# A two-layer decoder trunk on one core: the residual stream kept transposed, with weights as the stationary operand of the products that add to it

## The chip, the cores and the metric

The program runs on one core of one Trainium2 chip. The metric is the device time of one execution in microseconds (us). The kernel before takes 803.0 us, the median of three runs (802.51 to 804.0).

## The reference

Two consecutive layers act on a residual stream x of 256 tokens by 1,024 features, in float32. Each layer adds three branches to x, each behind an RMS norm with a gain: a token mixer, a cross-attention with 4 heads into 256 memory tokens, and a SwiGLU FFN of width 2,816. The mixer of layer 0 joins two kinds of sparse attention (8 heads each); that of layer 1 is grouped attention with a compressed, a selected and a window branch.

```
def rms_norm(x, gain):
    y = x * rsqrt(mean(x * x, axis=-1) + 1e-6)
    return y * gain

for each layer:
    x = x + mixer(rms_norm(x, norm_mix)) @ w_out
    x = x + mem_attention(rms_norm(x, norm_mem), rms_norm(mem, norm_mem_src)) @ mem_w_o
    g, u = split(rms_norm(x, norm_ffn) @ ffn_w_in)
    x = x + (silu(g) * u) @ ffn_w_out
```

## The kernel before

**Layout.** x lies in SBUF as two tiles (t = 0, 1) of 128 tokens on the partitions by 1,024 features. A product contracts over partitions, so a norm (`norm`, L619) transposes x: per half tile (512 features) TensorE makes four 128x128 transposes into PSUM, `evac_gain` (L608) multiplies the result by the gain on VectorE (tile `gv`), and splits it into a high part in fp32r (`move`: ScalarE or VectorE) and the low rest (`tt`: VectorE or GpSimd). The two parts stand in `hT`. The factor 1/rms is left out of the product's operand and applied to its result: ScalarE squares x with a running sum (tile `junk`), and `ms_root` (L599) makes mean and root of it. `mem_prep` (L1242) does the same with the memory tokens, in each layer anew, two tiles of 512 KB each.

**Products.** Each float32 product is three fp32r products (`mm3`, L565): high by high, high by low, low by high. `gemm` (L571) handles one tile of 128 tokens and a block of up to 512 weight columns: activations are the stationary operand (128x128), weights the moving one (up to 512 columns). Weights come by DMA in units of 256 rows by 512 columns (512 KB) into three raw buffers, and `pusher` (L395) splits each unit into high and low (tile `whl`, six units): the high part on ScalarE, the rest on VectorE. The products that add to x are `project` (L1375; twice 4 blocks of 128 rows), the end of `mem_attn` (L1292; 4 blocks) and the end of `ffn` (L1385; 22 blocks). Each of their results is 128 tokens by 512 features, and `residual` (L640) adds it to x on VectorE. `project` waits per half of the heads and per token tile for the attention's result (`finish`, L741, splits it, with `split`, L735), and `mem_attn` per pair of heads and per token tile.

**Order.** The program's order is made when it is built, by a planner: generators (`spawn`) yield operations, `Steps.run` (L84) takes the one that can start first by estimated costs and finish times (`Est`, L140), and operations that can run on several engines go to the one that would end first. Attention operations have rank 2, the main line of products rank 4, so the products fill what attention leaves free. Each engine then runs its list in that order. Buffers are slots (`Slots`, L263): two PSUM banks for products (`MM`), two each for scores, transposes and attention results, 23 slabs in SBUF. `main` (L1479) runs, per layer: mixer, keys of the memory (`mem_k`, L1267), `project`, `mem_attn`, `ffn`; the norms are spawned beside them and wait for the halves of x that they read.

The line that stops `project` before a token tile, and the adding of one result:

```
yield has(("oT", t, half), L + 1)
...
yield V.tensor_tensor(xs, ps, xs, op=OP.add)
```

Of the kernel before, what the change touches and what calls it, by code (L numbers as in the profile page):

```python
# [15 lines left out]
P = 128  # L16
D = 1024
# [122 lines left out]
class Est:  # L140
# [73 lines left out]
    class Engine:  # L214
# [21 lines left out]
        def cost(self, name, a, k, outs, ins):  # L236
# [3 lines left out]
            if self.n == "PE":  # L240
# [4 lines left out]
                if ins[0].dtype == F32R:  # L245
                    return n * (1 if n >= 256 else 4) * 0.000422
# [48 lines left out]
def trunk(ctx: ExitStack, tc: tile.TileContext, I, out):  # L295
# [42 lines left out]
    GV = Slots(est, tp, "gv", 2)  # L338
# [11 lines left out]

    x = [cp.tile([P, D], F32, name=f"x{t}") for t in range(NT)]
    xin = I["x"].rearrange("b (t p) d -> (b t) p d", p=P)
    rows = cp.tile([NG, P], F32, name="rows")
    posi = cp.tile([P, NT], I32, name="posi")

    def load_x(t, h, at):
        s = slice(512 * h, 512 * h + 512)
        nc.sync.dma_start(x[t][:, s], xin[t][:, s])
        est.note(x[t][:, s], est.wr, at, "D")

# [8 lines left out]
    def plan_block(key, w, col, n, K, base=0):  # L369
        plan_at[key] = len(plan)  # L370
        for k0 in range(0, K, 2):
            plan.append((w, col, n, base + k0))

    def load(i, lag=2.0):
        if i < len(plan):
            w, col, n, k0 = plan[i]
            raw, free = RW.take([P, 2, 512])
# [3 lines left out]
            nc.sync.dma_start(raw[:, :, :n], w[k0 * P:(k0 + 2) * P, col:col + n].rearrange("(k p) n -> p k n", p=P))  # L381
            raws[i] = (raw, free)

    class Unit:
        def __init__(self, i):
            n = plan[i][2]
            hl, self.free = WS.take([P, 2, 2, 512], F32R)
            self.hi, self.lo, self.n, self.left = hl[:, 0, :, :n], hl[:, 1, :, :n], n, NT
# [6 lines left out]
    def pusher():  # L395
        for i in range(len(plan)):
            yield WS.ready
            raw, rfree = raws.pop(i)
            u, n = Unit(i), plan[i][2]
            at[0] = i  # L400
            yield move(u.hi, raw[:, :, :n])
            yield V.tensor_tensor(u.lo, raw[:, :, :n], u.hi.bitcast(F32), op=OP.subtract)
# [13 lines left out]
    LASTC = 2  # L416
    for L in range(2):
# [3 lines left out]
        for half in (0, 1):  # L421
            for c in (0, 1):
                plan_block((L, "out", half, c), (I["ab_w_out"] if L == 0 else I["nsa_w_out"])[0], 512 * c, 512, 4, 4 * half)
        plan_block((L, "mq"), I["mem_w_q"][L], 0, 512, KD)
        plan_block((L, "mv"), I["mem_w_kv"][L], 512, 512, KD)
        for p in range(2):
            for c in (0, 1):
                plan_block((L, "mo", p, c), I["mem_w_o"][L], 512 * c, 512, 2, 2 * p)
# [4 lines left out]
        for k in range(0, KF - 2 * LASTC, 2):  # L433
            for c in (0, 512):
                plan.append((I["ffn_w_out"][L], c, 512, k))
        for c in (0, 512):
            for k in range(KF - 2 * LASTC, KF, 2):
                plan.append((I["ffn_w_out"][L], c, 512, k))
# [9 lines left out]
    load_x(0, 0, 3.5)  # L448
    nc.sync.dma_start(rows, I["gains"])
    est.note(rows, est.wr, 3.6, "D")  # L450
    load_x(0, 1, 4.4)
    clk["D"] = 3.3
    load(0, 1.1)
    load(1, 1.1)
    for h in range(2):
        clk["D"] += 0.73
        load_x(1, h, clk["D"] + 1.1)
    for i in range(2, RAWS):
        load(i, 1.1)
# [9 lines left out]
    gps, f = TP.take([P, 512])  # L469
    T.transpose(gps[:, :NG], rows, ident[:NG, :NG]).issue()  # L470
    gT = cp.tile([P, NG], F32, name="gT")
    V.tensor_copy(gT, gps[:, :NG]).issue()
    f()
# [12 lines left out]
    def tables():  # L486
# [21 lines left out]
        yield has(("mix0", 0), 2)  # L508
# [62 lines left out]
    def gemm(key, t, h, K, ev, need=None, part=None):  # L571
# [4 lines left out]
        for k0 in range(0, K, 2):  # L576
            u = yield from unit(plan_at[key] + k0 // 2)
            if need and k0 % 4 == 0:
                yield has(need[0], need[1] + 1 + k0 // 4)
# [11 lines left out]


    hT = [[cp.tile([P, KD, P], F32R, name=f"h{e}{t}") for e in range(2)] for t in range(NT)]
    junk = tp.tile([P, 512], F32, name="junk")
# [942 lines left out]
```

## Time and profile before

| | |
|---|---|
| median of three runs | 803.0 us (802.51, 803.0, 804.0) |
| profiled execution | 801.81 us, of which the span of the core is 800.1 us |
| granted clock of TensorE, mean | 0.996 |
| TensorE matmul busy | 766.0 us, 96% |
| VectorE busy | 537.5 us, 67% |
| ScalarE busy | 435.4 us, 54% |
| GpSimd busy | 130.9 us, 16% |
| read from HBM | 119.46 MB |

The span runs from the first instruction to the last; the profiled execution's own time is 1.7 us longer than it. Busy time of TensorE (PE) counts pipelined products and is no measure of its peak. PEld is its loading of stationary operands, DVE is VectorE, ACT ScalarE, POOL GpSimd, SPq the queue that issues DMAs. Most operations carry one line (L232), that of a helper, so groups are told apart by the names of their tiles: `mm` and `po` are PSUM banks with products, `sp` with scores, `tp` with transposes; `whl` are split weights, `h` the normed activations, `slab` other activations.

### The profile page before, as it was taken

The numbers are of one execution on the slowest core, as the hardware profiler recorded it, in microseconds if no ns is written. First come the engines' busy times: TensorE is split into PE (matmuls) and PEld (weight loads), VectorE is DVE, ScalarE is ACT, GpSimd is POOL, SyncE is SP. The second block draws the span as 40 slices with busy tenths as digits, with TensorE's granted clock in tenths as the row PEclk, the third lists the DMA queues.
The fourth block names the chain that finished last, engine by engine and source line by source line (L and its number), as shares of the span: only waits on it lengthen the run. The fifth ranks groups of instructions, "written<-read, shape, count | busy, mean of one in ns | idle before, by whom it ended". The sixth has DMA issues, their size and how long they took to land.

```text
span 800.1 us, 11833 instructions
## 1 busy us (share of the span) xinstructions
PE 766.0 (96%) x4259; PEld 632.1 (79%) x4259; DVE 537.5 (67%) x1096; ACT 435.4 (54%) x816; POOL 130.9 (16%) x192
## 2 busy tenths in 40 slices
PE   6878999999999999999999988999999999999998
PEld 5766777888888888888878776878897888889886
DVE  6779998877655655545727798887868565646541
ACT  5666887565544434444526788864656334435430
POOL 1544332110000000000007463230200000000000
PEclk9999999999999999999999999999999999999999
DMA  7613334635565553887315632033635656546761
GB/s 221 208 55 112 134 124 122 181 119 159 158 191 179 168 186 119 240 251 224 116 56 148 210 112 81 1 103 110 184 105 146 198 184 180 167 141 209 225 184 52
DMA packets 69482, 121.27 MB, mean 152 GB/s; under 512 B 8420, under 2 KB 15664, under 8 KB 69424
## 3 DMA queue, kind: packets, MB, share of 16 engines
q1 hardware_dynamic: 69392, 120.53, 49.2%
q8 instruction: 33, 0.54, 0.3%
q14 instruction: 25, 0.20, 0.1%
q0 software_dynamic: 32, 0.00, 0.0%
HBM read 119.46 MB, written 1.05 MB: 151 GB/s over the span
## 4 chain that ended last, share of the span: by engine, by line
PE 83%; DVE 7%; ACT 4%; DMA 2%; issue 2%; POOL 1%; SPq 0%; POOLq 0%; ACTq 0%; DVEq 0%
PE mm L232 61%; PE po L232 12%; PE tp L232 7%; PE sp L232 3%; DVE whl L232 2%; DMA raw<-in_ab_w_in 1%; DMA raw<-in_ffn_w_in 1%; ACT sn L232 1%; ACT whl L232 1%; DVE slab L232 1%; DVE acc L232 1%; ACT slab L232 1%; DVE sn L232 1%; DVE t L232 1%; POOL sn L232 1%
## 5 line engine op out<-in xcount | busy, mean ns | idle before, releaser
L232 PE MATMUL mm<-whl,h 128*128 128x512 f32 (+3 forms) x1776 | 397.8, 379 | 8.5 <-DVE whl L232 6.9
L232 PEld LDWEIGHTS mm<-whl,h 128*128 128x128 f32 x1776 | 310.8, 189 | 68.0 <-DVE whl L232 8.9
L232 DVE TENSOR_TENSOR whl<-raw,whl 128x1024 fp32r<-128x1024 f32 (+3 forms) x232 | 270.9, 1170 | 116.6 <-ACT whl L232 112.4
L232 ACT ACTIVATE whl<-raw 128x1024 fp32r<-128x1024 f32 (+3 forms) x211 | 213.2, 1014 | 160.1 <-DMA raw<-in_ffn_w_in 38.4
L232 PE MATMUL mm<-whl,slab 128*128 128x512 f32 (+1 forms) x840 | 200.2, 376 | 0.9 <-DVE x L232 0.8
L232 PEld LDWEIGHTS mm<-whl,slab 128*128 128x128 f32 x840 | 140.6, 189 | 27.7 <-issue 2.4
L232 PE MATMUL po<-whl,slab 128*128 128x512 f32 x264 | 68.4, 396 | 0.0
L232 ACT ACTIVATE slab<-tp 128x256 fp32r<-128x256 f32 (+2 forms) x63 | 28.3, 471 | 56.3 <-PE tp L232 55.9
L232 PEld LDWEIGHTS po<-whl,slab 128*128 128x128 f32 x264 | 49.4, 188 | 11.4
L232 POOL TENSOR_TENSOR rh<-vh,mhalf 128x1 f32<-128x1 f32 x12 | 9.5, 794 | 293.6 <-DVE vh L232 283.1
L232 ACT ACTIVATE sn<-sn,mx 128x128 f32<-128x128 f32 (+1 forms) x96 | 42.7, 447 | 6.9 <-DVE mx L232 6.5
L232 PE MATMUL tp<-ident,t 128*128 128x128 f32 x224 | 34.8, 277 | 2.7 <-DVE slab L232 2.3
L232 PE MATMUL tp<-ident,sn 128*128 128x128 f32 (+1 forms) x180 | 30.9, 281 | 4.8 <-POOL sn L232 3.8
L232 DVE TENSOR_TENSOR x<-mm,x 128x512 f32<-128x512 f32 x36 | 24.6, 687 | 16.0 <-PE mm L232 15.9
L232 PEld LDWEIGHTS tp<-ident,t 128*128 128x128 f32 x224 | 27.1, 142 | 9.6 <-DVE slab L232 2.8
L232 ACT ACTIVATE pt<-tp 128x512 f32<-128x512 f32 (+2 forms) x51 | 27.0, 536 | 13.7 <-PE tp L232 11.8
L232 DVE CUSTOM_DVE_ANT_0 sn<-sp,cm,rq 128x128 f32<-128x128 f32 (+1 forms) x80 | 30.5, 410 | 4.9 <-PE sp L232 3.8
L232 POOL TENSOR_TENSOR sn<-sn,rc 128x512 f32<-128x512 f32 (+2 forms) x27 | 25.5, 944 | 43.5 <-DVE rc L232 28.6
L232 ACT ACTIVATE t<-mm,rh 128x512 f32<-128x512 f32 (+1 forms) x26 | 17.0, 654 | 27.0 <-PE mm L232 27.0
L232 PEld LDWEIGHTS tp<-ident,sn 128*128 128x128 f32 (+1 forms) x180 | 20.7, 141 | 11.6 <-POOL sn L232 5.2
L232 ACT ACTIVATE t<-mm 128x512 f32<-128x512 f32 (+2 forms) x46 | 23.7, 553 | 10.0 <-PE mm L232 8.0
L232 DVE SCALAR_TENSOR_TENSOR t<-mm,rh,t 128x512 f32<-128x512 f32 (+1 forms) x24 | 16.9, 704 | 18.2 <-PE mm L232 18.2
(200 smaller groups left out, 676.3 us busy)
## 6 DMA issues: line engine op xcount, KB each, us to landing
raw<-in_ffn_w_in SPq DMA_DIRECT2D x80, 512.0 KB, 3.8
raw<-in_ffn_w_out SPq DMA_DIRECT2D x44, 512.0 KB, 4.5
raw<-in_ab_w_in SPq DMA_DIRECT2D x16, 512.0 KB, 3.9
raw<-in_mem_w_kv SPq DMA_DIRECT2D x16, 512.0 KB, 4.0
raw<-in_nsa_w_in SPq DMA_DIRECT2D x16, 512.0 KB, 3.7
raw<-in_ab_w_out SPq DMA_DIRECT2D x8, 512.0 KB, 3.6
raw<-in_mem_w_q SPq DMA_DIRECT2D x8, 512.0 KB, 4.2
raw<-in_mem_w_o SPq DMA_DIRECT2D x8, 512.0 KB, 3.6
```

Source lines behind the costliest of these rows:

```text
L232: return f(*a, **{q: v() if q in ("start", "stop") and callable(v) else v for q, v in k.items()})
```

## The change

x is kept as one tile of 128 features on the partitions by 8 blocks by 256 tokens; x, the memory tokens and the output are given in that layout in HBM (rearranged outside the kernel, once), and the gains also come transposed. A norm reads x directly: `gained` makes the high part (`move` with the gain as scale) and the rest (one `scalar_tensor_tensor`) per block of 256 columns. The sum of squares over features now runs over partitions: `squares` squares two blocks on ScalarE and adds them into `acc` (VectorE or GpSimd), and `ms_root` sums `acc` over partitions with two one-column products per norm. The memory's root is made once, in layer 0, and its tokens come in four pieces of 256 KB. The products that add to x take a 128x128 block of weights as the stationary operand and both token tiles (256 columns) as the moving one (`sums`): 1,632 products of 256 columns stand where 816 of 512 columns stood. Their weights come in units of 512 rows by 256 columns (`plan_banks`), also 512 KB, except those of the first part of the FFN's second product, which stay. A result is two blocks of features by 256 tokens, in one bank; the two head pairs of the memory's attention are now summed in PSUM. `project` and the memory's product wait for both token tiles of a half or pair. Two cost estimates of the planner are changed.

```diff
                 if ins[0].dtype == F32R:
-                    return n * (1 if n >= 256 else 4) * 0.000422
+                    return n * 0.00045 + 0.002
...
-            est.issue("D", [raw], [], 1.45 * n / 512)
+            est.issue("D", [raw], [], 2.4 * m * n / 1024)
...
+    def plan_banks(key, w, base):
+
+        plan_at[key] = len(plan)
+        for b in range(NB):
+            plan.append((w, 256 * b, 256, base, 4))
...
-    load_x(0, 0, 3.5)
+    clk["D"] = 1.2
+    nc.sync.dma_start(gT, I["gains_t"])
+    est.note(gT, est.wr, 3.4, "D")
+    for i in range(NB):
+        load_x(i)
+        if i < RAWS:
+            load(i, 1.1)
     nc.sync.dma_start(rows, I["gains"])
...
+    def sums(u, ps, k0, c0, hi, lo, first, last):
+
+
+        for k in range(2):
+            for j in range(2):
+                o, s = ps[:, j * SEQ:(j + 1) * SEQ], slice(c0 + j * P, c0 + (j + 1) * P)
+                whi, wlo = u.hi[:, k0 + k, s], u.lo[:, k0 + k, s]
+                yield T.matmul(o, whi, hi[:, k], start=first and k == 0 and j == 0, stop=False)
+                yield T.matmul(o, whi, lo[:, k], start=False, stop=False)
+                yield T.matmul(o, wlo, hi[:, k], start=False, stop=last and k == 1 and j == 1)
+                done("mm")
...
+    def gained(src, gain, hi, lo):
+
+        yield move(hi, src, gain)
+        yield V.scalar_tensor_tensor(lo, src, gain, hi.bitcast(F32), op0=OP.mult, op1=OP.subtract)
+
+    def squares(src, acc, first):
+
+        sq, f = yield from T2.get([P, 2, SEQ])
+        yield S.activation(sq, src, AF.Square)
+        if first:
+            yield tt(acc, sq[:, 0], sq[:, 1], OP.add)
+        else:
+            for j in range(2):
+                yield tt(acc, acc, sq[:, j], OP.add)
+        f()
+
+    def ms_root(key, acc, name):
...
+        ps, f = yield from TP.get([P, 512])
+        for t in range(NT):
+            yield T.matmul(ps[:, t:t + 1], acc[:, t * P:(t + 1) * P], one, start=True, stop=True)
+        yield V.tensor_scalar(v, ps[:, :NT], 1.0 / D, EPS, op0=OP.mult, op1=OP.add)
+        f()
         yield from pow_half(r, v)
...
-        for h in range(2):
-            yield has(("x", t, h), ver)
-            xs = x[t][:, 512 * h:512 * h + 512]
-            ps, f = yield from TP.get([P, 512])
-            for k in range(4):
-                yield T.transpose(ps[:, k * P:(k + 1) * P], xs[:, k * P:(k + 1) * P], ident)
-            yield from evac_gain(ps, f, hT[t][0][:, 4 * h:4 * h + 4], hT[t][1][:, 4 * h:4 * h + 4], gain[:, 4 * h:4 * h + 4])
-            done((key, t))
...
+    def norm(key, col, ver):
...
+        spawn(square())
+        for b in range(NB):
+            yield has(("x", b), ver)
+            for k in (2 * b, 2 * b + 1):
+                yield from gained(x[:, k], gT[:, col + k:col + k + 1], hT[0][:, k], hT[1][:, k])
+            done(key)
...
     def mem_prep(L):
...
+        for b in range(NB):
+            raw, rf = yield from T2.get([P, 2, SEQ])
+            nc.sync.dma_start(raw, I["mem"][:, 2 * b:2 * b + 2])
             est.note(raw, est.wr, clk["PE"] + 6.0, "D")
...
+            if L == 0:
+                yield from squares(raw, acc, b == 0)
             rf()
...
     def project(L):
         for half in range(2):
-            for t in range(NT):
-                yield has(("oT", t, half), L + 1)
-                hi, lo, f1, f2 = oT[t, half]
-                for c in range(2):
-                    yield from gemm((L, "out", half, c), t, lambda k: (hi[:, k, :], lo[:, k, :]), 4, residual(c))
...
+            for b in range(NB):
+                yield MM.ready
+                ps, free = MM.take([P, 512])
+                u = yield from unit(plan_at[L, "out", half] + b)
+                for i in range(2):
+                    yield has(("oT", L, half, i), 2)
+                    (hi, _), (lo, _) = oT[L, half][i]
+                    yield from sums(u, ps, 2 * i, 0, hi, lo, i == 0, i == 1)
+                u.free()
+                spawn(residual(b, ps, free))
...
+        for b0 in (0, 2):
+            held = []
+            for p in range(2):
+                yield has(("mo", L, p), 2)
+                for b in (b0, b0 + 1):
```

## Rows read from the trace of the kernel before

**Rows 1.** The page: engines, and the chain that ended last, by engine.

```profile
PE 766.0 (96%) x4259; PEld 632.1 (79%) x4259; DVE 537.5 (67%) x1096; ACT 435.4 (54%) x816; POOL 130.9 (16%) x192
PE 83%; DVE 7%; ACT 4%; DMA 2%; issue 2%; POOL 1%; SPq 0%; POOLq 0%; ACTq 0%; DVEq 0%
```

**Rows 2.** Stretches: PE, PEld, DVE, ACT, POOL busy; clock, DMA share, GB/s.

```profile
186.00:203.00 17.00, 16.41 (x79) 13.07 (x79) 15.69 (x23) 8.81 (x13) 0.00 (x0) 1.00 0.69 213
460.00:500.00 40.00, 34.35 (x297) 28.55 (x295) 35.43 (x138) 33.94 (x105) 20.97 (x26) 0.96 0.29 96
725.00:732.00 7.00, 7.00 (x62) 7.00 (x62) 3.64 (x6) 3.31 (x7) 0.00 (x0) 1.00 0.61 203
```

**Rows 3.** Whom TensorE waited for: us in total, times, longest.

```profile
PE tp L232 <- DVE slab L232: 5.6, 5, 2.0
```

**Rows 4.** The chain that ended last, in order of time: start, us, what.

```profile
203.24 0.44 PE tp L232 x4
203.68 13.75 PE mm L232 x60
...
724.38 8.25 PE mm L232 x70
...
790.69 5.61 PE po L232 x24
```

**Rows 5.** Groups of TensorE by shape: count, busy us, mean ns of one, idle before.

```profile
L232 PE MATMUL tp<-ident,x 128*128 128x128 f32 x96 | 15.8, 292 | 1.4 <-DMA x<-in_x 1.4
L232 PE MATMUL mm<-whl,slab 128*128 128x256 f32 x192 | 26.3, 285 | 0.0
L232 PE MATMUL sp<-kbd,slab 128*128 128x30 f32 x32 | 4.3, 265 | 0.0
```

**Rows 6.** Instructions in order of time at the program's start, TensorE.

```profile
3.99 1.06 PE L232 MATMUL tp<-ident,x 128*128 128x128 f32 x4
```

**Rows 7.** The same where layer 0's attention ends: start, us, engine.

```profile
138.86 0.66 PE L232 MATMUL po<-pt,bv 128*64 128x128 f32 x8
...
139.83 0.58 ACT L232 ACTIVATE slab<-po 128x512 fp32r<-128x512 f32 x1
139.96 1.23 DVE L232 TENSOR_TENSOR whl<-raw,whl 128x1024 fp32r<-128x1024 f32 x1 [0.30 <-ACT whl L232]
141.10 0.68 DVE L232 TENSOR_TENSOR slab<-po,slab 128x512 fp32r<-128x512 f32 x1
```

**Rows 8.** Output products after attention's end: layer 0 (139.4 to 151.9), layer 1 (543.9 to 561.3).

```profile
L232 PE MATMUL mm<-whl,slab 128*128 128x512 f32 x48 | 12.2, 402 | 0.0
...
L232 PE MATMUL mm<-whl,slab 128*128 128x512 f32 x69 | 17.0, 399 | 0.0
```

**Rows 9.** Groups of VectorE, ScalarE and GpSimd by shape, columns as in rows 5.

```profile
L232 DVE TENSOR_TENSOR x<-mm,x 128x512 f32<-128x512 f32 x36 | 24.6, 687 | 16.0 <-PE mm L232 15.9
L232 DVE SCALAR_TENSOR_TENSOR acc<-sn,iw,acc 128x256 f32<-128x256 f32 x7 | 3.7, 526 | 0.3 <-ACT sn L232 0.3
L232 DVE TENSOR_TENSOR slab<-po,slab 128x256 fp32r<-128x256 f32 x8 | 3.2, 418 | 3.7 <-ACT slab L232 3.7
...
L232 ACT ACTIVATE slab<-tp,kv 128x256 fp32r<-128x256 f32 x8 | 3.5, 473 | 5.5 <-PE tp L232 5.5
...
L232 POOL TENSOR_TENSOR acc<-acc,cmi 128x256 f32<-128x256 f32 x1 | 0.7, 737 | 3.3 <-DVE acc L232 3.3
```

**Rows 10.** One operation of VectorE beside GpSimd, and alone, in order of time.

```profile
206.75 0.69 DVE L232 CAST whl<-raw 128x1024 fp32r<-128x1024 f32 x1
...
467.70 1.73 POOL L232 TENSOR_TENSOR t<-t,t 128x512 fp32r<-128x512 f32 x1 [0.49 <-ACT t L232]
468.22 1.76 DVE L232 CAST whl<-raw 128x1024 fp32r<-128x1024 f32 x1
```

**Rows 11.** DMA: issues of the memory tokens in layer 1; landing times by size.

```profile
480.70 4.04 SPq L1246 DMA_DIRECT2D t<-in_mem  x2
...
raw<-in_ffn_w_in SPq DMA_DIRECT2D x8, 256.0 KB, 2.8
```

More of the change, by code (lines that the diff above doesn't have):

```diff
@@ new lines, in trunk @@
+    hT = [cp.tile([P, KD, SEQ], F32R, name=f"h{e}") for e in range(2)]
+    def hsel(t):
+        return lambda k: (hT[0][:, k, t * P:(t + 1) * P], hT[1][:, k, t * P:(t + 1) * P])
+    def gained(src, gain, hi, lo):
[10 more added lines that the diff above has]
+        f()
@@ L1288, in mem_k @@
         for t in range(NT):
-            yield has(("mT", L, t))
-            yield from gemm((L, "mk"), t, msel(t), KD, ev)
+            yield from gemm((L, "mk"), t, msel(t), KD, ev, ("mT", L))
     def mem_attn(L):
@@ L1345, in mem_pv @@
             ptf()
[L1346 to L1349 removed]
+            if (L, p) not in mo:
+                mo[L, p] = None
+                mo[L, p] = (yield from SL.get([P, 2, SEQ], F32R)), (yield from SL.get([P, 2, SEQ], F32R))
+            yield lambda: mo[L, p] is not None
+            yield from split(po, *(mo[L, p][e][0][:, :, t * P:(t + 1) * P] for e in range(2)))
+            pof()
+            done(("mo", L, p))
         def ev_v(p):
             def ev(ps, free, t):
[L1353 removed]
+                yield move(vm[:, t, 2 * p:2 * p + 2].rearrange("p h d -> p (h d)"), ps, (yield from root("mem", t))[1])
                 free()
@@ L1358, in mem_attn @@
         for t in range(NT):
[L1359 removed]
+            yield from gemm((L, "mq"), t, hsel(t), KD, ev_q, ("mem", L))
         for p in range(2):
@@ L1449, in ffn @@
-        n = 0
-        for i in range(KF // 2 - LASTC):
+        ps = []
+        for R in (MM, MM, PV, PV):
+            yield R.ready
+            ps.append(R.take([P, 512]))
+        n = plan_at[L, "fo"]
+        for i in range(KF // 2 - 2):
             yield has(("aT", L, i), 2)
             for c in range(2):
-                u = yield from unit(i0 + n)
+                u = yield from unit(n)
                 n += 1
-                for t in range(NT):
-                    yield from fo(u, i, c, t)
+                for b in range(2):
+                    yield from sums(u, ps[2 * c + b][0], 0, 256 * b, aT[i][0][0], aT[i][1][0], i == 0, False)
+                u.free()
@@ L1457, in ffn @@
             for e in range(2):
                 aT[i][e][1]()
-        for t in range(NT):
-            m = n
-            for c in range(2):
-                for i in range(KF // 2 - LASTC, KF // 2):
-                    yield has(("aT", L, i), 2)
-                    yield from fo((yield from unit(i0 + m)), i, c, t)
-                    m += 1
-                spawn(residual(c)(ps[t, c][0], ps[t, c][1], t))
-        for i in range(KF // 2 - LASTC, KF // 2):
+        for b in range(NB):
+            u = yield from unit(n + b)
+            for i in range(KF // 2 - 2, KF // 2):
+                yield has(("aT", L, i), 2)
+                yield from sums(u, ps[b][0], 2 * (i - KF // 2 + 2), 0, aT[i][0][0], aT[i][1][0], False, i == KF // 2 - 1)
+            u.free()
+            spawn(residual(b, *ps[b]))
```

271 lines of the change are left out of this document (110 added, 161 removed).

## The prediction

> **What bounds the kernel now.** I read the page's engines and its chain first, then the stretches, then the chain piece by piece, and the groups of each engine for prices. The page [rows 1] shows TensorE busy for 96% of the span, and the chain that ended last lies on TensorE for 83%. So a product or transpose taken from TensorE in a stretch where it is never idle is time won, and work taken from another engine is not. Where is it not full? The chain in order of time [rows 4] shows the FFN as products end to end, broken only by groups of four transposes. In layer 1's attention (460 to 500) it is busy 34.35 us of 40, so 5.65 us are idle [rows 2]. At the end of the memory's attention and the start of the FFN (186 to 203) it is nearly full, but VectorE is busy 15.69 us of 17 there: the engine to watch. The output products left after an attention's end [rows 8] show how much the main line has in hand when the attention stops: 48 of 96 in layer 0, 69 of 96 in layer 1.
>
> **The change part by part.** The sum is made against the profiled execution, 801.8 us, 1.2 us under the median of 803.0; I move the result up by that.
>
> *Transposes of norms.* The code has 16 transposes per norm in six norms; the group of x has these 96 [rows 5]. A group of four costs the chain 0.44 us [rows 4]. Five norms (both memory norms, both FFN norms, layer 1's mixer norm) lie in full stretches: 5 x 4 groups x 0.44 = **-8.8 us**. The sixth opens the program, see below. The memory tokens' 2 x 16 transposes go too. Layer 1's four groups lie where output products fill up: 4 x 0.44 = **-1.8**. Layer 0's four I cost at nothing: they lie ahead of an attention whose end sets when the second half of its output products can run.
>
> *Start.* Four transposes (1.06 us, [rows 6]) and a 128x512 multiply out of PSUM (0.69, as the residual's [rows 9]) no longer stand between the first x and its first product: **-1.8**. Against it, all of x (1 MB) must now land for the first token tile; before, half. Lower bound 0, upper bound twice the gain; I take the path's length.
>
> *Narrower products.* 816 products of 512 columns become 1,632 of 256. The old ones are priced by the FFN's last 24: 5.61/24 = 0.234 us each, 190.7 in all [rows 4]. The new by the 70 of 256 columns in the FFN's narrow block: 8.25/70 = 0.1179, 192.3 in all [rows 4]. Difference **+1.6**. The ends: 0 (two halves were nowhere cheaper than the whole), and the dearest row of this shape, 26.3/192 = 0.137 us [rows 5], which gives 223.6 and +32.9. That row's products lie among other work, so I stay with the unbroken run. There the loading of stationary operands is busy 7.00 us of 7.00 [rows 2]: no reserve is left.
>
> A rule of the Trainium skill speaks against this step: "TensorE: Matmul & The Clock Gate", section "Back-to-back issue gap", gives as the sustained spacing of load and product pairs 81 ns at 128 columns and 131 ns at 512. By it two narrow products cost at least 162 ns against 131, an estimate of 816 x 0.031 = +25 us for this term. The trace does not bear it out: 234 ns at 512.
>
> *Sums of squares.* Seven roots (six norms, the memory once) put 14 float32 products of one column on TensorE. The nearest row has 30 columns: 4.3/32 = 0.134 us [rows 5]; 14 x 0.134 = **+1.9**, between 0 and the price of a group of transposes per root (7 x 0.44 = 3.1).
>
> *Waiting for both token tiles.* In layer 0, 48 products remain when the attention ends, the whole second half [rows 8]; token tile 0's 24 hid the wait for tile 1. Now nothing does. After the last attention product (about 139.5), the copy started at 139.83 and the rest at 141.10, behind a weight split of 1.23 us [rows 7]. With half pieces (0.42 for the rest, [rows 9]; about as much for the copy) the first operand is ready at 140.7 without a split ahead, 141.5 with one: 1.2 to 2.0, taken **+1.6**. In layer 1, 69 remain, so 21 of the first half (21 x 0.234 = 4.9 us) cover the same 2 us. The memory's product waits likewise for tile 1's first pair, behind which the second pair's products run: 0.3 per layer, **+0.6**, between 0 and the 2.0 above per layer. The second pair is covered by 24 narrow products (2.8 us).
>
> *The norm after the last product.* The next gemm needs the last bank only after 18 products: 18 x 13.75/60 = 4.1 us [rows 4]. The bank needs the addition (0.69), high part (0.47) and two rests (2 x 0.53, [rows 9]): 2.2 us. It fits with 1.9 us in hand, one weight split but not two. For six boundaries I put in **+1.5**; alone it would be 0, the upper end is a rival below. VectorE loses 8 of 40 additions (5.5 us), 32 multiplies and their rests, and gains 64 rests (33.7) and up to 49 additions of 256 columns (49 x 0.418 = 20.5); about even. ScalarE's 64 scaled copies (30 us) replace squares with sums and unscaled copies of the same order, at 54% busy [rows 1].
>
> *Memory tokens.* SP now issues four pieces in place of two, among the weight loads behind it [rows 11]. Each piece lands in about 2.8 us [rows 11], but the planner reckons 6 us for each and takes the next one only after it. So layer 1's keys may start earlier (a quarter suffices) yet end no earlier. I put **-0.5**; between -5.65 (all idle time of 460 to 500 filled) and +1.7 (12 us later at that stretch's idle share, 14%). Weight units with rows of 1 KB in place of 2 KB cost nothing by the same landing time, half of a unit in 2.8 us against 2.8 us of products per unit, with three raw buffers ahead; if that cover is gone, about a microsecond per FFN.
>
> Sum: -8.8 - 1.8 - 1.8 + 1.6 + 1.9 + 1.6 + 0.6 + 1.5 - 0.5 = **-5.7**, so 796.1 for the profiled execution and **797.3 us** by the median.
>
> **The rivals.**
>
> *More comes back than the transposes.* The planner's costs are changed: 0.232 us in place of 0.216 for a product of 512 columns, nearer to the rows' 0.229 to 0.234, and a slower DMA. If instructions are then placed so that the three waits I added (3.7 us) vanish, and half of the 5.6 us in which transposes wait for VectorE [rows 3], the time is 797.3 - 3.7 - 2.8 = **790.8**. For it: the idle time exists. Against it: that order is the planner's and cannot be read from this trace.
>
> *The last bank's norm comes late (slower).* Per bank of 2.83 us of products, VectorE has a split (1.23), an addition (0.69), two rests (1.05) and two sums (0.84): 3.8 us, 1.0 too much. Over four banks it is 3.9 us behind, the operand comes 3.9 + 2.2 - 4.1 = 2.0 us late, at five boundaries 10 us; less the 1.5 already counted: **805.8**. It decides from (5.7 + 1.5)/5 = 1.4 us per boundary on. For it: VectorE's load at 186 to 203 [rows 2]. Against it: the sums may go to GpSimd, idle there [rows 2], at 0.74 us each [rows 9]. But one VectorE operation that takes 0.69 us alone took 1.76 beside a GpSimd one [rows 10], and the new rests read two operands from SBUF where the old multiply read PSUM. The Trainium skill, "SBUF — State Buffer", section "SBUF: two separate sides", tells of one port pair that a GpSimd operation and such a VectorE operation take in turn, whole; the trace agrees.
>
> *Weight loads set the pace (slower).* With the load queue full, any dearer load shows 1,632 times. At 0.137 us [rows 5] the time is 797.3 + 31 = **828**; from 0.1214 us on (5.7/1,632 more) the gain is gone. Against it: the unbroken run. The skill's spacing rule above, if it held, would end here, too.
>
> *Nothing to measure.* If the bounds above fall on the bad side (root products 3.1, layer 0's wait 2.0, memory waits 4.0, memory tokens +1.7), it is 797.3 + 7.2 = **804.5**.
>
> **How the numbers follow.** A measurement of this kernel can tell about 0.2% from no change, so faster means under 801.4 and slower over 804.6. Chances: the forecast 0.48, more coming back 0.27, nothing to measure 0.11, the late norm 0.11, weight loads 0.03. The first two are faster (0.75), the last two slower (0.14). The range 788 to 804 holds the forecast, most of the second and half of the third case.
>
> **What would show it.** Right: no transposes of x or of memory tokens, 1,632 products of 256 columns at 0.116 to 0.120 us in the FFN's second product, norm boundaries without idle time, a wait of 1 to 2 us before layer 0's second half. Wrong: TensorE waiting for `h` at each boundary, narrow products above 0.121 us apart, root products that stop TensorE, or a span under 790 with the attention stretches shortened.

## The result, and the profile after

The changed kernel takes **810.2 us** (median of 4 runs, 809.52 to 812.63) beside 802.8 of the kernel before on the same chip: a ratio of 1.0094, 95% interval 1.0070 to 1.0119. It is slower by 7.3 us, where 797.3 had been forecast. The profiled execution takes 810.7 us with a span of 809.0, beside 800.1 before.

The page of the changed kernel, its engines and the engines of the chain that ended last, beside [rows 1]:

```profile
PE 766.7 (95%) x4974; PEld 669.4 (83%) x4974; DVE 545.8 (67%) x1092; ACT 423.6 (52%) x803; POOL 166.6 (21%) x227
PE 82%; DVE 8%; ACT 5%; issue 2%; POOL 1%; DMA 1%; SPq 0%; ACTq 0%; POOLq 0%; DVEq 0%
```

TensorE is busy for as long as before (766.7 us against 766.0), in a span 8.9 us longer. So what was added is idle time; what the transposes gave back was taken up by other work on TensorE. The starts of the stages, from TensorE's instructions in order of time, say where (us):

| stage begins with | before | changed | late by | added in the stage before it |
|---|---|---|---|---|
| memory queries, layer 0 | 152.02 | 158.09 | 6.07 | 6.07 |
| FFN, layer 0 | 199.18 | 204.22 | 5.04 | -1.03 |
| FFN's second product, layer 0 | 325.54 | 331.18 | 5.64 | 0.60 |
| mixer, layer 1 | 388.49 | 394.74 | 6.25 | 0.61 |
| memory queries, layer 1 | 561.38 | 568.47 | 7.09 | 0.84 |
| FFN, layer 1 | 608.23 | 614.56 | 6.33 | -0.76 |
| FFN's second product, layer 1 | 734.57 | 741.49 | 6.92 | 0.59 |
| end of the span | 800.1 | 809.0 | 8.9 | 1.98 |

Two thirds are lost before layer 0's memory queries. Stretches of the kernel before, which show where (columns as in [rows 2]):

```profile
80.00:120.00 40.00, 38.22 (x247) 29.82 (x247) 36.25 (x122) 33.72 (x87) 14.90 (x20) 1.00 0.38 129
480.00:520.00 40.00, 36.74 (x334) 30.48 (x335) 34.46 (x150) 32.47 (x110) 12.65 (x17) 1.00 0.11 41
```

The same stretches of the changed kernel:

```profile
80.00:120.00 40.00, 30.37 (x199) 23.15 (x198) 33.84 (x136) 29.40 (x84) 15.65 (x22) 0.96 0.31 100
480.00:520.00 40.00, 35.21 (x318) 28.47 (x317) 32.60 (x144) 31.59 (x107) 18.68 (x23) 0.96 0.20 67
```

Beside layer 0's attention 9.6 of 40 us are idle on TensorE, where 1.8 were. What is missing there stands in the order of time. First SP's issues of the memory tokens, two tiles in the kernel before:

```profile
66.41 0.34 SPq L1246 DMA_DIRECT2D t<-in_mem  x1
85.46 0.41 SPq L1246 DMA_DIRECT2D t<-in_mem  x1
```

and four pieces in the changed kernel, the last one requested 19.5 us later than the last tile before:

```profile
70.16 0.42 SPq L1267 DMA_DIRECT2D t<-in_mem  x1
77.53 0.46 SPq L1267 DMA_DIRECT2D t<-in_mem  x1
89.13 0.50 SPq L1267 DMA_DIRECT2D t<-in_mem  x1
104.91 0.50 SPq L1267 DMA_DIRECT2D t<-in_mem  x1
```

Then TensorE's products of the memory keys (`mm<-whl,slab` of 512 columns), of the output projection behind them (`mm<-slab,whl`), and the first of the memory queries:

```profile
84.92 1.32 PE L233 MATMUL mm<-whl,slab 128*128 128x512 f32 x5
87.32 0.46 PE L233 MATMUL mm<-whl,slab 128*128 128x512 f32 x1
90.05 0.86 PE L233 MATMUL mm<-whl,slab 128*128 128x512 f32 x3
91.38 1.02 PE L233 MATMUL mm<-whl,slab 128*128 128x512 f32 x3 [0.47 <-ACT slab L233]
101.79 1.40 PE L233 MATMUL mm<-whl,slab 128*128 128x512 f32 x5
103.97 0.49 PE L233 MATMUL mm<-whl,slab 128*128 128x512 f32 x1
117.26 0.50 PE L233 MATMUL mm<-whl,slab 128*128 128x512 f32 x1
...
133.43 3.02 PE L233 MATMUL mm<-slab,whl 128*128 128x256 f32 x24
137.40 3.26 PE L233 MATMUL mm<-slab,whl 128*128 128x256 f32 x25 [0.95 <-DVE x L233]
140.85 17.40 PE L233 MATMUL mm<-slab,whl 128*128 128x256 f32 x143
158.09 2.22 PE L233 MATMUL mm<-whl,h 128*128 128x512 f32 x9
```

The keys come in steps of six: 5+1 products, 3+3, then nothing for 9 us, 5+1, and nothing for 13 us. Each piece of the memory tokens (256 rows of features, both token tiles) feeds six products of token tile 0; tile 1's 24 come only after tile 0's last. So when the fourth piece has come, at 117, 30 of 48 products still stand before the output projection. All 192 products of the projection then lie behind the attention, whose last product starts at 132.26. In the kernel before the first tile's tokens carried 24 products, from 95.70 on, and the second tile's the other 24. The attention itself ended 6.6 us earlier than before (its last product started at 138.86 there, [rows 7]), but from that product to the memory queries it is now 25.8 us, where it was 13.2.

The list of waits does not name this. On TensorE in the changed kernel it has, for whom it waited, us in total, times and longest:

```profile
PE mm L233 <- ACT whl L233: 9.4, 2, 8.6
PE tp L233 <- POOL sn L233: 8.6, 6, 3.2
PE mm L233 <- DVE x L233: 2.3, 3, 1.0
PE tp L233 <- ACT mvm L233: 2.0, 2, 1.0
```

The order of TensorE's instructions is fixed when the program is built. Where the planner had no keys to place, it placed attention instructions, and the idle time is written down to what those waited for (`sn`, the attention's own). The first row is the start, up to the first weights. The third was 0.8 us in two waits in the kernel before; two of its three waits here, 0.66 us each, stand at the starts of the FFN, see below.

### The profile page after: what moved, and what is told of

Its sections match the earlier page's. It is cut to its first block, busy times and chain, and to the rows that moved or that the text cites. A ratio compares the mean times of both kernels' runs of the same rounds, so it can differ in the third digit from the quotient of the medians.

```text
span 809.0 us, 13277 instructions
## 1 busy us (share of the span) xinstructions
PE 766.7 (95%) x4974; PEld 669.4 (83%) x4974; DVE 545.8 (67%) x1092; ACT 423.6 (52%) x803; POOL 166.6 (21%) x227
## 4 chain that ended last, share of the span: by engine, by line
PE 82%; DVE 8%; ACT 5%; issue 2%; POOL 1%; DMA 1%; SPq 0%; ACTq 0%; POOLq 0%; DVEq 0%
PE mm L233 62%; PE po L233 12%; PE tp L233 5%; PE sp L233 3%; DVE whl L233 2%; DVE sn L233 1%; ACT sn L233 1%; ACT t L233 1%; ACT whl L233 1%; ACT slab L233 1%; DVE slab L233 1%; POOL sn L233 1%; DVE h L233 1%; DVE x L233 1%; DMA raw<-in_nsa_w_in 1%
## 5 line engine op out<-in xcount | busy, mean ns | idle before, releaser
L233 PE MATMUL mm<-whl,h 128*128 128x512 f32 (+3 forms) x1776 | 404.1, 382 | 19.5 <-ACT whl L233 9.4
L233 ACT ACTIVATE whl<-raw 128x1024 fp32r<-128x1024 f32 (+3 forms) x197 | 198.9, 1011 | 153.0 <-PE mm L233 67.2
L233 PE MATMUL mm<-slab,whl 128*128 128x256 f32 x1104 | 138.8, 284 | 1.0 <-DVE x L233 1.0
L233 PEld LDWEIGHTS mm<-slab,whl 128*128 128x128 f32 x1104 | 134.8, 192 | 1.6 <-DVE x L233 1.2
L233 PE MATMUL po<-slab,whl 128*128 128x256 f32 x528 | 66.6, 283 | 0.0
L233 PEld LDWEIGHTS po<-slab,whl 128*128 128x128 f32 x528 | 64.8, 192 | 0.0
L233 PE MATMUL mm<-whl,slab 128*128 128x256 f32 (+1 forms) x288 | 57.9, 333 | 0.5 <-ACT slab L233 0.5
L233 POOL TENSOR_TENSOR acs<-acs,t 128x256 f32<-128x256 f32 x42 | 41.1, 978 | 32.3 <-ACT t L233 30.5
L233 PEld LDWEIGHTS mm<-whl,slab 128*128 128x128 f32 x288 | 40.6, 190 | 4.8 <-issue 1.2
L233 DVE SCALAR_TENSOR_TENSOR h<-x,gT,h 128x256 fp32r<-128x256 f32 x48 | 33.1, 699 | 7.3 <-ACT h L233 7.1
L233 PEld LDWEIGHTS tp<-ident,sn 128*128 128x128 f32 (+1 forms) x180 | 20.6, 145 | 19.9 <-POOL sn L233 10.7
L233 DVE CAST whl<-raw 128x1024 fp32r<-128x1024 f32 (+1 forms) x35 | 24.3, 695 | 14.5 <-PE mm L233 10.6
```

The costliest lines, as they stand in the source:

```text
L233: return f(*a, **{q: v() if q in ("start", "stop") and callable(v) else v for q, v in k.items()})
```

## The experiments

Kernels were compared with the kernel before on the same chip; each ratio has its 95% interval. The planner reorders everything behind an edit, so I first give what that alone is worth.

**How far the order alone moves the time.** One edit to the kernel before changes nothing but a constant of the planner, the other puts the changed kernel's two cost constants into it:

```diff
-WAIT = 0.03
+WAIT = 0.04
```
```diff
-                    return n * (1 if n >= 256 else 4) * 0.000422
+                    return n * 0.00045 + 0.002
...
-            est.issue("D", [raw], [], 1.45 * n / 512)
+            est.issue("D", [raw], [], 2.4 * n / 512)
```

> The kernel before, with the span within which the planner takes instructions by rank set to 0.04 us in place of 0.03: no work changed, only the order where two instructions are close. If the order alone is worth under a microsecond: 801.5 to 803.5 us. If it is worth two or three (then single edits of that size above tell little): outside that.

Measured: 805.0 us, ratio 1.0035 (1.0021 to 1.0049).

> The kernel before with the planner's two constants of the changed kernel. If they place the work worse by themselves: 804.5 to 806 us, as the changed kernel gained 2.6 us without them. If it was only the order of one kernel that happened to fall better: 801 to 804.

Measured: 799.6 us, 0.9970 (0.9959 to 0.9981), below both ranges. The reverse, the changed kernel with the constants of before:

> The changed kernel with the planner's two constants of the kernel before (cost of a product, cost of a weight load's issue). Theory (they are not what cost the time): 807.5 to 811.5 us. Rival (the new constants place the work worse): under 806.

Measured: 807.2 us, 1.0061 (1.0043 to 1.0080), between the two ranges. By these three runs order alone is worth 2.5 to 3 us either way. The new constants made one kernel faster and the other slower, so they are no cause by themselves, and a single edit that moves the time by under 3 us shows nothing unless the trace shows it in its place.

**The memory tokens.** First a remedy that failed: two pieces of 512 KB, both requested at once, and 25 slabs in place of 23.

```diff
+        got = []
+        for b in range(0, NB, 2):
+            got.append((yield from T4.get([P, 4, SEQ])))
+            nc.sync.dma_start(got[-1][0], I["mem"][:, 2 * b:2 * b + 4])
...
         for b in range(NB):
-            raw, rf = yield from T2.get([P, 2, SEQ])
-            nc.sync.dma_start(raw, I["mem"][:, 2 * b:2 * b + 2])
...
+            raw, rf = got[b // 2][0][:, 2 * (b % 2):2 * (b % 2) + 2], got[b // 2][1]
...
```

> The changed kernel, with the memory tokens fetched in two pieces of 512 KB that are both requested at once (in place of four of 256 KB, one after the other), and 25 slabs in place of 23 (the room that the old gain buffers left). My theory (the memory keys start late because their tokens come in four pieces in series and slabs are short, so that the main line has nothing to run beside the attentions): TensorE's idle time in the stretch 80 to 120 falls from 9.6 us to under 3, that of layer 1's attention by some 2 us, and the time is 802 to 804.5 us. Rival (the main line would stop at the output projection instead, or the planner's new constants are the cause): memory keys earlier, idle time moved behind them, 808.5 to 811 us.

Measured: 812.1 us, 1.0133 (1.0118 to 1.0149). The rival was right in kind, and the time lies 1.1 us above its range. The last keys and the first output products on TensorE:

```profile
108.03 0.39 PE L233 MATMUL mm<-whl,slab 128*128 128x512 f32 x1
126.82 0.38 PE L233 MATMUL mm<-slab,whl 128*128 128x256 f32 x1
```

Now the keys are done at 108, and the main line stands for 18 us before the projection, which needs the attention's first half of both tiles. The memory queries start at 158.17, as late as in the changed kernel. Early is as bad as late: the keys' products are what fills the attention, and must lie beside it.

Next, layer 0's memory tokens left out of either kernel, with as many products from another operand:

```diff
-        spawn(mem_prep(0), 2)
...
-            yield from gemm((L, "mk"), t, msel(t), KD, ev, ("mT", L))
+            yield from gemm((L, "mk"), t, msel(t) if L else hsel(t), KD, ev, ("mT", L) if L else None)
...
```

> The changed kernel without the memory tokens in layer 0: nothing is loaded, scaled or squared for them there, and layer 0's memory keys and values are made from the block's own normed input (as many products as before, other numbers). Theory (in layer 0 the time went to the memory tokens: four small pieces in series and short of slabs, for which the main line waits while the attention can't fill TensorE): the memory queries of layer 0 start 7 to 9 us earlier than in the changed kernel (at 149 to 151 us in place of 158.1), and the time is 800.5 to 803 us. Rival (layer 0 lost its time at the start and in the attention itself): 2 to 3 us earlier, as much as the same cut brings the kernel before, and 806 to 808 us.

Measured: 805.4 us, 1.0030 (1.0018 to 1.0042).

> The kernel before, with the same cut: no memory tokens in layer 0, keys and values of its memory made from the block's own input. Both theories: the memory's transposes and copies go, the queries start 2 to 3 us earlier (at 149 to 150 us in place of 152), 799 to 800.5 us.

Measured: 802.3 us, 0.9998 (0.9990 to 1.0007). The cut is worth 5 us to the changed kernel and nothing to the kernel before. The levels expected were missed, by 2.4 and 1.8 us, and the changed kernel's time lies nearer to the rival's range; the place and the difference between the kernels are the theory's. The memory queries start at 148.37, 9.7 us earlier, and at 150.35 in the kernel before, 1.7 us earlier. Of the 9.7 us, 3.9 are lost again between layer 1's mixer and its memory queries; there this version makes the sum of squares of the memory, which it leaves out of layer 0.

Then the wait itself. The changed kernel's keys are made piece by piece for both tiles, so that 12 products follow each piece (and with 25 slabs in place of 23):

```diff
-        for t in range(NT):
-            yield from gemm((L, "mk"), t, msel(t), KD, ev, ("mT", L))
+        banks = []
+        for t in range(NT):
+            yield MM.ready
+            banks.append(MM.take([P, 512]))
+        for b in range(NB):
+            u = yield from unit(plan_at[L, "mk"] + b)
+            yield has(("mT", L), b + 1)
+            for t in range(NT):
+                for j in range(2):
+                    hi, lo = msel(t)(2 * b + j)
+                    yield from mm3(banks[t][0], hi, lo, u.hi[:, j], u.lo[:, j], b + j == 0, b == NB - 1 and j == 1)
+                u.used()
...
```

> The changed kernel with nothing but the memory keys made piece by piece for both token tiles (and 25 slabs in place of 23, which that order needs). If waiting for the last piece is the cost by itself: 5 to 8 us less than the changed kernel, 801.5 to 804.5 us. If the gain came with the additions on VectorE: 806 to 809 us.

Measured: 803.3 us, 1.0016 (1.0006 to 1.0026), 6.3 us less by the ratios. The stretch beside layer 0's attention (columns as in [rows 2]):

```profile
80.00:120.00 40.00, 35.09 (x228) 26.86 (x229) 37.66 (x138) 31.94 (x88) 15.83 (x24) 1.00 0.38 125
```

The first memory queries of that run on TensorE:

```profile
152.36 6.13 PE L233 MATMUL mm<-whl,h 128*128 128x512 f32 x26
```

4.7 us of idle time are gone from the stretch, and the queries start 5.7 us earlier, where the whole span is 6.2 us shorter. The first three pieces of the tokens come no earlier here, but the fourth is requested 4.7 us earlier than in the changed kernel:

```profile
100.16 1.13 SPq L1267 DMA_DIRECT2D t<-in_mem  x1
```

So this run alone does not tell the order of the products from the two slabs more. Two runs further below do, both with 23 slabs and with the additions of squares on VectorE: with the old order of the keys 807.0 us, with the new one 801.7, 5.0 us less by the ratios. Their fourth piece is requested at about the same time (108.87 and 108.05), the memory queries start 2.7 us earlier (157.77 and 155.06), and 2.9 us more are won between layer 1's mixer and its memory queries. Last, the wait put into the kernel before:

```diff
-            yield has(("mT", L, t))
+            yield has(("mT", L, 0))
+            yield has(("mT", L, 1))
```

> The kernel before, with one wait more and nothing else: the memory keys of token tile 0 wait for the tokens of tile 1 too, as the changed kernel's must. If that wait is the cost: 6 to 12 us more, 808 to 814 us, with TensorE idle beside both attentions and the memory keys of layer 0 ending after 128 us in place of 118.6. If the cost is in the changed kernel's own smaller pieces: under 805.5 us.

Measured: 815.5 us, 1.0171 (1.0157 to 1.0185): 13.4 us from one wait, 1.5 us above the range expected. The same stretch:

```profile
80.00:120.00 40.00, 33.27 (x216) 25.91 (x214) 34.32 (x122) 31.14 (x85) 11.35 (x17) 0.91 0.40 129
```

TensorE in order of time before and after the gap, and at the first memory queries:

```profile
94.94 0.94 PE L232 MATMUL mm<-whl,h 128*128 128x512 f32 x3
111.83 3.29 PE L232 MATMUL mm<-whl,slab 128*128 128x512 f32 x13
...
159.52 0.86 PE L232 MATMUL mm<-whl,h 128*128 128x512 f32 x3
```

The main line stands from 95.9 to 111.8, and the queries start at 159.52, 7.5 us later than before; layer 1 loses 5.5 us more between its mixer and its memory queries. So the wait costs time where it is put in and gives time back where it is taken out. How the 5.7 us of layer 0 divide between the order of the keys and the earlier fourth piece stays open.

**The wait for both tiles before the output projection**, put into the kernel before:

```diff
-                yield has(("oT", t, half), L + 1)
+                yield has(("oT", 0, half), L + 1)
+                yield has(("oT", 1, half), L + 1)
```

> The kernel before, whose output projection waits for both token tiles of a half of the heads before its first product. My theory (this wait was sized about right and is not where the time went): within 2 us of the kernel before, 802.5 to 804.5 us, the wait showing only after layer 0's attention. Rival (the wait for both tiles starves the main line): 806 to 809 us, with TensorE idle beside both attentions.

Measured: 803.5 us, 1.0019 (1.0010 to 1.0028), so 1.5 us: about the +1.6 of the forecast, though no more than order alone.

**The additions of squares.** On VectorE alone, in `squares`:

```diff
-            yield tt(acc, sq[:, 0], sq[:, 1], OP.add)
+            yield V.tensor_tensor(acc, sq[:, 0], sq[:, 1], op=OP.add)
...
-                yield tt(acc, acc, sq[:, j], OP.add)
+                yield V.tensor_tensor(acc, acc, sq[:, j], op=OP.add)
```

> The changed kernel, only with the additions of squares on VectorE alone, without the early table load. Theory (what the earlier run with both gained came from the additions on GpSimd, which hold up VectorE at every norm and not at the start alone): 805 to 807 us. Rival (it came from the table load): 808.5 to 810.

Measured: 807.0 us, 1.0065 (1.0047 to 1.0084). With an early table load besides:

```diff
+    warm = cp.tile([P, 1], F32, name="warm")
+    S.activation(warm, one, AF.Square).issue()
```

> The changed kernel with two edits at the start: a one-element Square at the beginning brings ScalarE's table load ahead of the input, and the additions of squares go to VectorE only. My theory (the start lost about 6 us against the forecast: late table load, VectorE slowed beside GpSimd's additions): the first 424-column block ends 3 to 4 us earlier (22.5 to 23.5 us in place of 26.5) and the time is 806 to 807.5 us. Rival 1 (what the start loses is absorbed in the first attention's idle time): the block ends earlier, the time stays 809 to 811. Rival 2 (weights set the pace of the start): the block still ends at 26 or later.

Measured: 805.9 us, 1.0052 (1.0039 to 1.0066); the first block ended at 26.6, not 23. Neither time says much beside what order alone does, but the first run's gain has its place in the trace: 1.5 us between the memory queries and the FFN (44.6 in place of 46.1), in layer 0 and in layer 1 alike, and 0.6 us in the FFN's first part (126.4 in place of 127.0), again in both. TensorE at the FFN's start in the changed kernel:

```profile
204.22 7.83 PE L233 MATMUL mm<-whl,h 128*128 128x512 f32 x33 [0.66 <-DVE x L233]
...
216.40 6.92 PE L233 MATMUL mm<-whl,h 128*128 128x512 f32 x29 [0.45 <-ACT t L233]
```

The groups of the norm there (count, busy us, mean ns of one, idle before):

```profile
L233 POOL TENSOR_TENSOR acs<-acs,t 128x256 f32<-128x256 f32 x42 | 41.1, 978 | 32.3 <-ACT t L233 30.5
L233 DVE SCALAR_TENSOR_TENSOR h<-x,gT,h 128x256 fp32r<-128x256 f32 x48 | 33.1, 699 | 7.3 <-ACT h L233 7.1
```

The FFN's start with the additions on VectorE:

```profile
202.38 5.66 PE L233 MATMUL mm<-whl,h 128*128 128x512 f32 x24
```

And the groups of that run:

```profile
L233 DVE SCALAR_TENSOR_TENSOR h<-x,gT,h 128x256 fp32r<-128x256 f32 x48 | 22.4, 476 | 4.9 <-ACT h L233 4.9
L233 DVE TENSOR_TENSOR acs<-acs,t 128x256 f32<-128x256 f32 x42 | 17.4, 415 | 0.0
```

The waits at the FFN's start, 0.66 and 0.45 us per layer, are gone. Most of the rest of the 1.5 us is another wait that is gone, inside the memory's attention of the changed kernel:

```profile
175.46 0.63 PE L233 MATMUL tp<-ident,sn 128*128 128x128 f32 x4 [0.97 <-ACT mvm L233]
```

In the 6 us before it GpSimd adds no squares, and the kernel before waits 1.24 us at the same place, so no run shows that it belongs to the additions; order may have moved it. VectorE takes on 49 additions and sheds 33.1 - 22.4 = 10.7 us of rests, so each rest, on which the next product waits, is ready sooner: a rest took 223 ns longer on average while GpSimd made the additions. The trace agrees with the rule of the shared port pair (the Trainium skill, "SBUF — State Buffer", section "SBUF: two separate sides").

**The start.** The 424-column products of the first block in the changed kernel, on TensorE:

```profile
8.56 0.72 PE L233 MATMUL mm<-whl,h 128*128 128x424 f32 x1 [8.56 <-ACT whl L233]
9.63 2.49 PE L233 MATMUL mm<-whl,h 128*128 128x424 f32 x6 [0.36 <-DVE whl L233]
13.46 2.49 PE L233 MATMUL mm<-whl,h 128*128 128x424 f32 x6 [1.33 <-DVE whl L233]
16.92 2.13 PE L233 MATMUL mm<-whl,h 128*128 128x424 f32 x5 [0.97 <-DVE whl L233]
```

Six of them span 2.49 us, the last 0.72 long, so they stand (2.49 - 0.72) / 5 = 0.354 us apart: 424 columns at 1.2 GHz. In the kernel before it was 0.19 from 12 us on, as in these:

```profile
14.69 1.43 PE L232 MATMUL mm<-whl,h 128*128 128x424 f32 x6 [0.63 <-DVE whl L232]
```

I tried to bring TensorE to its higher level with transposes of the identity ahead:

```diff
+    wps, f = TP.take([P, 512])
+    for _ in range(28):
+        T.transpose(wps[:, :P], ident, ident).issue()
+    f()
```

> The changed kernel with 28 transposes of the identity, whose result nobody reads, on TensorE before its first product. My theory (the transposes of the norm, which the change removed from the start, had brought TensorE to its higher clock: in the changed kernel the 424-column products stand 0.354 us apart until 23 us, in the kernel before 0.194 from 12 us on; 27 products x 0.16 = 4.3 us): products 0.194 us apart from the first units on, the first block ends at 22 to 23 us in place of 27.8, and the time is 804 to 806 us where the changed kernel has about 809.5. Rival (the weights' splits set the pace of the start): the block still ends after 25.5 us and the time is 808 to 810.

Measured: 808.9 us, 1.0082 (1.0063 to 1.0101), the block ending at 28.1 as the rival had it. The second and third unit of that run:

```profile
9.19 1.50 PE L233 MATMUL mm<-whl,h 128*128 128x424 f32 x6 [0.62 <-DVE whl L233]
13.00 2.49 PE L233 MATMUL mm<-whl,h 128*128 128x424 f32 x6 [2.31 <-DVE whl L233]
```

The first products are fast, but TensorE then waits 2.31 us for VectorE's split, and the next six are at the lower level again. With all three edits:

> The changed kernel with the 28 transposes ahead, the early table load, and all additions of squares on VectorE. If the two effects are separate (about -4 and -3.5): 801 to 803.5 us. If they are the same microseconds of the start: 804.5 to 806.5.

Measured: 805.4 us, 1.0039 (1.0023 to 1.0055): the start's repair adds nothing that can be told from order.

**The width.** The kernel before with its residual products cut to 256 columns:

```diff
...
+        for z in range(2):
+            s = slice(256 * z, 256 * z + 256)
+            yield T.matmul(o[:, s], hh, whi[:, s], start=start and z == 0, stop=False)
+            yield T.matmul(o[:, s], hh, wlo[:, s], start=False, stop=False)
+            yield T.matmul(o[:, s], hl, whi[:, s], start=False, stop=stop and z == 1)
...
```

> The kernel before, with only its residual products (output projection, memory output, second product of the FFN) split into two products of 256 columns each: 1,632 in place of 816, activations still stationary, residual stream not transposed. My theory (the width was mis-sized, a narrow product costs 0.120 us and not 0.1179): 0.120 us between products in the second FFN product, and 802.8 + 5.3 = 808 us. Rival (the width is nearly free as forecast, and the 0.120 us of the changed kernel belongs to weights as stationary operand): 0.117 to 0.118 us, and 803 to 804.5 us.

Measured: 805.3 us, 1.0042 (1.0030 to 1.0055). The time is between the two theories, the spacing is the rival's: its last piece of the chain (start, us, what), with 0.118 us per product:

```profile
794.20 5.67 PE po L232 x48
```

The same piece of the changed kernel, 5.77 / 48 = 0.120:

```profile
799.46 5.77 PE po L233 x48
```

And with half of the stationary columns, and with them half of the rows of the result, left out in most of the second FFN product of the changed kernel:

```diff
-                yield T.matmul(o, whi, hi[:, k], start=first and k == 0 and j == 0, stop=False)
...
+                    for a, b in ((whi, hi), (whi, lo), (wlo, hi)):
+                        yield T.matmul(o[:64], a[:, :64], b[:, k], start=False, stop=False)
```

> The changed kernel, in whose second FFN product all but the first and the last few products load 64 of 128 stationary columns and write 64 of 128 rows (half of that sum is left out). If loading the weights sets the 0.120 us of a narrow product: 0.107 to 0.115 us apart. If the 256 moving columns set it: 0.119 to 0.120.

Measured: 802.9 us (one run), and in the chain, first the changed kernel, then this one:

```profile
779.30 2.88 PE po L233 x24
```

```profile
778.03 2.72 PE po L233 x24
```

2.88 / 24 = 0.120 and 2.72 / 24 = 0.113 us, with 256 moving columns in both. So the moving columns do not set the last 7 ns of the 0.120. That the load of the stationary operand does is likely and not shown: the run halves the rows written as well. Why weights as stationary operand are dearer than activations (0.120 against 0.118) stays open.

**Versions that put the parts together.** Additions on VectorE, and keys piece by piece (the edits shown above, with 23 slabs):

> The changed kernel with additions of squares on VectorE alone, and the memory keys made piece by piece for both token tiles: after each piece of the memory tokens 12 products, in place of all of tile 0 first, which needs all four pieces. Theory (the main line waits for the memory tokens' last piece before it can do tile 1's half of the work): 3 to 5 us less than the run with the additions alone had (807.0), so 802 to 804 us. Rival (the attentions' own length sets the end, the main line only waits elsewhere): 806 to 808.

Measured: 801.7 us, 1.0003 (0.9990 to 1.0016), just below the first range. With the constants of before and the table load:

> The last kernel with the planner's constants of the kernel before and the early table load too. If the parts add up (constants -2.6, table -1): 798.5 to 801 us, less than either kernel. If they share their microseconds: 802 to 804.

Measured: **800.0 us**, 0.9972 (0.9962 to 0.9982), faster than either kernel. It is no faster than the kernel before with other constants (0.9970), so the transposed stream has here drawn level, not won. The first block piece by piece as well (25 slabs):

```diff
-        for t in range(NT):
-            yield from gemm((0, "s"), t, h[t], KD, ev_small, "mix0")
...
+        for b in range(NB):
+            u = yield from unit(plan_at[0, "s"] + b)
+            yield has("mix0", b + 1)
+            for t in range(NT):
...
```

> The best kernel so far (VectorE additions, memory keys piece by piece, constants of before, early table load), with the first block made piece by piece for both token tiles as well: 12 products per weight unit as it arrives, in place of 6, and 25 slabs. If the start lacks work per weight unit: the first block ends at 19 to 21 us in place of 23.2, and the time is 797.5 to 799.5 us. If VectorE, behind on splits and norms, sets it: the block ends after 22 and the time stays at 799.5 to 801.

Measured: 801.4 us, 0.9992 (0.9981 to 1.0003). The block ends at about 20 us, 3 us earlier, and no time comes of it: the place is the first theory's, the time lies just above the second's range. What the start loses is not seen on the path.

## Why the prediction was wrong

The sign was wrong: faster had 0.75, and the time lies above the range. Term by term:

- **Memory tokens, forecast -0.5: this step failed.** It saw that the planner fetches the four pieces one after the other, and that a quarter suffices to begin. But it priced their lateness by layer 1's idle share (14%, [rows 2]), as if the main line's other products went on meanwhile. There are none: the keys are the only products that fill the attention, in a fixed order. The last piece was requested 19.5 us later than the last tile before, and after it 30 of 48 products had to follow, in place of 24. Measured +5.7 us in layer 0 (by the run with keys piece by piece and two slabs more), for which the term had nothing. The bound of +1.7 was wrong for the same reason.
- **The norm after the last product, forecast +1.5.** With the additions on GpSimd TensorE waits 0.66 + 0.45 us at the FFN's start in each layer, 2.2 in both; the run without them is 4.2 us shorter in these stretches, of which the rest has no place that the additions explain. The mechanism was the one of the rival "the last bank's norm comes late", at under half its price (10 us) even by the larger figure. GpSimd's addition took 0.978 us against the 0.737 of [rows 9].
- **Narrower products, forecast +1.6.** 1,632 x 0.120 = 195.8 against the forecast's 190.7 for the old ones: +5.1. Right in kind; 0.1179 was the price with activations stationary, which the run with cut columns shows again (0.118). The term is far below the +25 us estimated by the rule that had stood against this step (the Trainium skill, "TensorE: Matmul & The Clock Gate", section "Back-to-back issue gap").
- **Start, forecast -1.8.** The first block ended 5.6 us later, but the main line reached the memory keys earlier than before (84.92 against 95.70) and then waited for tokens, and a block that ended 3 us earlier brought no time. No run shows it on the path: 0 in place of the gain.
- **Transposes of norms (-8.8), root products (+1.9), the output projection's wait (+1.6).** Transposes of x are gone, and the run with the wait alone puts it at 1.5 us. A root's four instructions hold TensorE for 0.37 us (211.88 to 212.25 in layer 0's FFN), so 7 x 0.37 = 2.6.

With the measured sizes in place of the forecast ones (tokens 5.7 for -0.5, norm 2.2 for 1.5, products 5.1 for 1.6, start 0 for -1.8, roots 2.6 for 1.9) the sum is -5.7 + 6.2 + 0.7 + 3.5 + 1.8 + 0.7 = +7.2 us, beside 8.9 by the spans and 7.3 by the medians. That it comes so close is partly luck: order alone moves 2.5 to 3 us, and -8.8 for the transposes was not measured apart. None of the four rivals had the main cause: the slower ones looked at norms and weight loads, and the wait for the last piece stood inside a term of half a microsecond.

## What to carry to other kernels

When a change turns an operand's pieces the other way (features in place of tokens), ask of every consumer how many products it can run after the first piece and how many are left after the last. Here 24 became 30, the last piece came later, and a loop order (all of tile 0, then tile 1) that had cost nothing cost 5 to 6 us. Products that fill an attention have to lie beside it: too early loses as much as too late. And where a planner lays out the order, measure first how far a change of nothing but the order moves the time; here it was 2.5 to 3 us, and effects under that were trusted only where the trace showed them in their place in both layers.

## What the runs showed of the hardware that I had not expected

- At the start of the changed kernel products stand 0.354 us apart, at the lower of TensorE's two levels, while the granted clock of the stretch 8 to 20 us reads 1.00. In the run with the transposes ahead the same stretch reads 0.64, though its first products were faster. So in this stretch the 1.00 of the record is no evidence of the higher level; the spacing of products shows the lower one. First the stretch of the changed kernel:

```profile
8.00:20.00 12.00, 8.78 (x23) 6.72 (x23) 11.68 (x32) 9.43 (x17) 5.99 (x7) 1.00 0.62 186
```

  Then that of the run with transposes:

```profile
8.00:20.00 12.00, 7.99 (x24) 6.32 (x25) 11.64 (x35) 8.97 (x17) 6.23 (x7) 0.64 0.57 186
```

- In the kernel before the first block's products were at the higher level, 0.19 us apart, from 12 us on, in the changed kernel only from about 23.5 us on. With 28 transposes ahead the first unit of six took 1.50 us in place of 2.49. That the norm's own transposes had done the same in the kernel before is likely and not shown: its waits at the start differ, too.
- Halving the stationary columns and the rows of the result from 128 to 64 took 7 ns off a product of 256 moving columns (0.120 to 0.113 us).
